# A column-sum kernel: loads folded to four rows and passed along a 24-row ring, shrinking loads at the end, 60 drains ahead of the vector work, and the last three rows read in two column blocks

## The chip, the cores and the metric

The kernel runs on one core of a Trainium2 chip. The metric is the device time of one execution in microseconds (us). Each run also lists its span, which is the time from the first to the last instruction that the profile counts, and the mean clock granted to the tensor engine. The time is about 2 us longer than the span (1.82 us in the profiled run of before). The difference between the two is called "outside the span" below.

In profile lines PE is the tensor engine's matmuls, PEld its weight loads, DVE VectorE, ACT ScalarE, and SP the sync engine, which issues all transfers here. SPq is the issuing itself.

## The reference

```python
def setup_inputs():
    batch, seq, dim = 32, 1024, 2048
    return {"grad_output": np.random.randn(batch, seq, dim).astype(np.float32)}

def reference(grad_output):
    return np.sum(grad_output, axis=(0, 1)).astype(np.float32)
```

A matrix of 32,768 x 2,048 floats, 268.4 MB, is read once and summed down to 2,048 numbers. On the chip 128 matrix rows, one for each partition, make one "row" of 1 MB in this document. The matrix has 256 such rows.

## The kernel before

```python
ROWS = 8
TAIL = (4, 2, 1)
# first column, columns, column group of 32 in PE's output
PIECES = ((0, 512, 1), (512, 512, 2), (1024, 512, 3), (1536, 256, 0), (1792, 256, 0))
...
io_pool = ctx.enter_context(tc.tile_pool(name="io", bufs=3))
nc.vector.memset(ones[:], 1.0)
...
def add_piece(b, src, stop=False):          # sum over the 128 partitions, into PSUM
    nc.tensor.matmul(sums[b], lhsT=ones[:], rhs=src, start=(b not in started), stop=stop)
...
for t in range(n_bulk):                     # 31 loads of 8 rows
    T = io_pool.tile([P, ROWS * D], fp32, tag="T", name=f"t{t}")
    nc.sync.dma_start(out=T[:], in_=src)
    n = ROWS * D // 2
    while n >= D:                           # 8 -> 4 -> 2 -> 1 rows on VectorE
        ...
        nc.vector.tensor_add(out=T[:, :n], in0=T[:, :n], in1=T[:, n : 2 * n])
        n //= 2
    if t:
        nc.vector.tensor_add(out=acc[:], in0=acc[:], in1=T[:, :D])

for i, m in enumerate(TAIL):                # 4, 2, 1 rows go to PE as they are
    nc.sync.dma_start(out=T[:, at * D : (at + m) * D], in_=src)
    for j in range(m):
        add_row(T[:, (at + j) * D : (at + j + 1) * D])
    at += m
add_row(acc[:])
for b, (lo, n, g) in enumerate(PIECES):     # the last row in five column pieces
    nc.sync.dma_start(out=dst, in_=flat[row : row + P, lo : lo + n])
    add_piece(b, dst, stop=True)
    if b in (0, 2, 4):
        nc.scalar.copy(out=res[:, lo : lo + n], in_=sums[b])
    else:
        nc.vector.tensor_copy(out=res[:, lo : lo + n], in_=sums[b])
nc.sync.dma_start(out=out[None, :], in_=res)
```

Lines are left out of this cut, also where no ... stands, and comments are added. The whole kernel follows.

Of the kernel before, what the change touches and what calls it, by code (L numbers as in the profile page):

```python
# [1 line left out]

# [4 lines left out]

P = 128
ROWS = 8  # L10
TAIL = (4, 2, 1)


PIECES = ((0, 512, 1), (512, 512, 2), (1024, 512, 3), (1536, 256, 0), (1792, 256, 0))


@with_exitstack
def kernel(
    ctx: ExitStack,
    tc: tile.TileContext,  # L20
    grad_output: bass.AP,
    out: bass.AP,
):
    nc = tc.nc
    fp32 = mybir.dt.float32
    D = out.shape[-1]
    flat = grad_output.rearrange("b s d -> (b s) d")
    R = flat.shape[0]
    n_bulk = (R // P - sum(TAIL) - 1) // ROWS
    assert (n_bulk * ROWS + sum(TAIL) + 1) * P == R  # L30

    io_pool = ctx.enter_context(tc.tile_pool(name="io", bufs=3))
    const_pool = ctx.enter_context(tc.tile_pool(name="const", bufs=1))
    psum_pool = ctx.enter_context(tc.tile_pool(name="psum", bufs=1, space=bass.MemoryType.PSUM))

    ones = const_pool.tile([P, 1], fp32)
    nc.vector.memset(ones[:], 1.0)  # L37
    warm = const_pool.tile([1, 1], fp32)
    nc.scalar.copy(out=warm[:], in_=ones[0:1, :])  # L39
    acc = const_pool.tile([P, D], fp32)  # L40
    sums = []
    for b, (lo, n, g) in enumerate(PIECES):
        bank = psum_pool.tile([P, 512], fp32, tag=f"ps{b}", name=f"ps{b}")
        sums.append(bank[32 * g : 32 * g + 1, :n])

    started = set()

    def add_piece(b, src, stop=False):
        nc.tensor.matmul(sums[b], lhsT=ones[:], rhs=src, start=(b not in started), stop=stop)  # L49
        started.add(b)  # L50

    def add_row(src):
        for b, (lo, n, g) in enumerate(PIECES):
            add_piece(b, src[:, lo : lo + n])

    row = 0
    for t in range(n_bulk):
        T = io_pool.tile([P, ROWS * D], fp32, tag="T", name=f"t{t}")
        src = flat[row : row + P * ROWS].rearrange("(p m) d -> p (m d)", p=P)
        nc.sync.dma_start(out=T[:], in_=src)  # L60
        row += P * ROWS
        n = ROWS * D // 2
        while n >= D:
            if t == 0 and n == D:
                nc.vector.tensor_add(out=acc[:], in0=T[:, :n], in1=T[:, n : 2 * n])  # L65
            else:
                nc.vector.tensor_add(out=T[:, :n], in0=T[:, :n], in1=T[:, n : 2 * n])  # L67
            n //= 2
        if t:
            nc.vector.tensor_add(out=acc[:], in0=acc[:], in1=T[:, :D])  # L70

    T = io_pool.tile([P, ROWS * D], fp32, tag="T", name="tail")
    at = 0
    for i, m in enumerate(TAIL):
        src = flat[row : row + P * m].rearrange("(p m) d -> p (m d)", p=P)
        nc.sync.dma_start(out=T[:, at * D : (at + m) * D], in_=src)
        row += P * m
        for j in range(m):
            add_row(T[:, (at + j) * D : (at + j + 1) * D])
        at += m  # L80
    add_row(acc[:])

    res = acc[0:1, :]
    for b, (lo, n, g) in enumerate(PIECES):
        dst = T[:, at * D + lo : at * D + lo + n]
        nc.sync.dma_start(out=dst, in_=flat[row : row + P, lo : lo + n])
        add_piece(b, dst, stop=True)
        if b in (0, 2, 4):
            nc.scalar.copy(out=res[:, lo : lo + n], in_=sums[b])  # L89
        else:  # L90
            nc.vector.tensor_copy(out=res[:, lo : lo + n], in_=sums[b])  # L91
    nc.sync.dma_start(out=out[None, :], in_=res)


# [1 line left out]
_INS = ['grad_output']  # L96
_OUTS = [((2048,), 'float32')]


# [23 lines left out]
```

## Time and profile before

| | before |
|---|---|
| time, median of the first 3 runs | 629.85 us (629.35 to 630.53) |
| span of the profiled run (timed 630.02) | 628.2 us |
| DMA packets, share of 16 engines' span | 99.0% |
| VectorE busy | 87% |
| last input landed, from the span's start | 624.16 us |

An input counts as landed when the last of the 16 DMA engines has reported its part of it. These times come from the semaphore records in the trace.

These are lines of the page of before: the busy times of part 1, the queues of part 3 (packets, megabytes, share of the 16 engines' time) and the chain of part 4.

```profile
span 628.2 us, 430 instructions
PE 10.6 (2%) x90; PEld 3.8 (1%) x90; DVE 547.6 (87%) x126; ACT 3.0 (0%) x5; POOL 0.2 (0%) x4
...
q1 hardware_dynamic: 5618, 268.45, 99.0%
q14 instruction: 1, 0.01, 0.0%
...
DMA 69%; DVE 28%; PE 2%; issue 0%; ACT 0%; SPq 0%; ACTq 0%
```

The DMA engines work nearly all the time (99.0%), and 268.4 MB pass through them whatever the kernel does. There is also one packet of another kind, on q14, which the page calls "instruction": 8,192 bytes at 240.15 us. It is called a fetch below and is taken to be VectorE's.

This is the view of groups by shape for VectorE in before. Its columns are the line, engine, operation, tiles, shapes and count, then the busy time and the mean ns of one, then the idle time before them.

```profile
L67 DVE TENSOR_TENSOR t<-t 128x8192 f32<-128x8192 f32 x31 | 269.5, 8692 | 71.8 <-DMA t<-in_grad_output_dram 71.8
L67 DVE TENSOR_TENSOR t<-t 128x4096 f32<-128x4096 f32 x31 | 137.2, 4425 | 1.1
L70 DVE TENSOR_TENSOR acc<-acc,t 128x2048 f32<-128x2048 f32 x30 | 68.8, 2292 | 1.0
L67 DVE TENSOR_TENSOR t<-t 128x2048 f32<-128x2048 f32 x30 | 68.8, 2292 | 1.0
```

One load costs VectorE 8.69 + 4.43 + 2.29 + 2.29 = 17.7 us, and a load lands every 19.35 us, so VectorE waits for the DMA with every load.

This is the end of the timeline of before (start, duration, engine, line, operation, tiles, count, and in brackets the idle time and what ended it).

```profile
617.62 2.29 DVE L67 TENSOR_TENSOR t<-t 128x2048 f32<-128x2048 f32 x1
617.63 4.98 PE L49 MATMUL ps<-tail,ones 128*1 128x512 f32 x50
619.95 2.29 DVE L70 TENSOR_TENSOR acc<-acc,t 128x2048 f32<-128x2048 f32 x1
622.42 1.05 PE L49 MATMUL ps<-acc,ones 128*1 128x512 f32 x10
623.28 1.63 PE L49 MATMUL ps<-tail,ones 128*1 128x512 f32 x10
624.34 1.57 ACT L89 COPY acc<-ps 1x512 f32<-1x512 f32 x3 [622.12 <-PE ps L49]
624.38 1.13 DVE L91 COPY acc<-ps 1x512 f32<-1x512 f32 x2 [2.14 <-PE ps L49]
625.93 0.33 SPq L92 DMA_DIRECT2D out_dram<-acc  x1
```

The accumulator is complete at 619.95 + 2.29 = 622.24 us. PE adds it, then the last row, whose last piece landed at 624.16, and ends at 624.91. Of the five result copies ScalarE makes three in a row. The output goes out at 625.93.

### The profile page before, as it was taken

The numbers are of one execution on the slowest core, as the hardware profiler recorded it, in microseconds if no ns is written. First come the engines' busy times: TensorE is split into PE (matmuls) and PEld (weight loads), VectorE is DVE, ScalarE is ACT, GpSimd is POOL, SyncE is SP. The second block draws the span as 40 slices with busy tenths as digits, with TensorE's granted clock in tenths as the row PEclk, the third lists the DMA queues.
The fourth block names the chain that finished last, engine by engine and source line by source line (L and its number), as shares of the span: only waits on it lengthen the run. The fifth ranks groups of instructions, "written<-read, shape, count | busy, mean of one in ns | idle before, by whom it ended". The sixth has DMA issues, their size and how long they took to land.

```text
span 628.2 us, 430 instructions
## 1 busy us (share of the span) xinstructions
PE 10.6 (2%) x90; PEld 3.8 (1%) x90; DVE 547.6 (87%) x126; ACT 3.0 (0%) x5; POOL 0.2 (0%) x4
## 2 busy tenths in 40 slices
PE   0000000000000000000000000000000000000006
PEld 0000000000000000000000000000000000000002
DVE  0578988889888899888898888988889988899886
ACT  0000000000000000000000000000000000000000
POOL 0000000000000000000000000000000000000000
PEclk9999999999999999999999999999999999999999
DMA  9999999999999999999999999999999999999996
GB/s 401 413 455 401 467 401 467 401 467 401 467 401 467 401 467 401 463 405 459 409 459 409 455 413 455 413 455 413 451 417 451 417 446 421 438 430 426 442 403 266
DMA packets 5619, 268.45 MB, mean 427 GB/s; under 512 B 625, under 2 KB 881, under 8 KB 1265
## 3 DMA queue, kind: packets, MB, share of 16 engines
q1 hardware_dynamic: 5618, 268.45, 99.0%
q14 instruction: 1, 0.01, 0.0%
HBM read 268.44 MB, written 0.01 MB: 427 GB/s over the span
## 4 chain that ended last, share of the span: by engine, by line
DMA 69%; DVE 28%; PE 2%; issue 0%; ACT 0%; SPq 0%; ACTq 0%
DMA t<-in_grad_output_dram 64%; DVE t L67 25%; DMA tail<-in_grad_output_dram 5%; DVE acc L70 4%; PE ps L49 2%; ACT acc L89 0%; SPq L60 0%; ACTq L118 0%
## 5 line engine op out<-in xcount | busy, mean ns | idle before, releaser
L67 DVE TENSOR_TENSOR t<-t 128x8192 f32<-128x8192 f32 (+2 forms) x92 | 475.4, 5167 | 73.9 <-DMA t<-in_grad_output_dram 71.8
L70 DVE TENSOR_TENSOR acc<-acc,t 128x2048 f32<-128x2048 f32 x30 | 68.8, 2292 | 1.0
L49 PE MATMUL ps<-tail,ones 128*1 128x512 f32 (+1 forms) x80 | 10.0, 627 | 614.3 <-DMA tail<-in_grad_output_dram 614.3
L49 PEld LDWEIGHTS ps<-tail,ones 128*1 128x1 f32 x80 | 3.5, 97 | 620.3 <-issue 617.4
L89 ACT COPY acc<-ps 1x512 f32<-1x512 f32 (+1 forms) x3 | 1.5, 506 | 622.2 <-PE ps L49 622.1
L91 DVE COPY acc<-ps 1x512 f32<-1x512 f32 (+1 forms) x2 | 1.1, 548 | 2.2 <-PE ps L49 2.1
L65 DVE TENSOR_TENSOR acc<-t 128x2048 f32<-128x2048 f32 x1 | 2.3, 2292 | 0.0
L39 ACT ACT_TABLE_LOAD x1 | 1.3, 1283 | 0.7 <-PEq L107 0.7
L49 PE MATMUL ps<-acc,ones 128*1 128x512 f32 (+1 forms) x10 | 1.1, 507 | 0.0
L37 DVE MEMSET ones<- 128x1 f32 x1 | 0.1, 59 | 0.8 <-PEq L107 0.8
L49 PEld LDWEIGHTS ps<-acc,ones 128*1 128x1 f32 x10 | 0.4, 82 | 0.4 <-DVE acc L70 0.2
L39 ACT COPY warm<-ones 1x1 f32<-1x1 f32 x1 | 0.2, 190 | 0.0
L107 POOL MEMSET const-bfloat16-1.0<- 128x1 bf16 x1 | 0.1, 101 | 0.0
L107 POOL MEMSET const-uint8-127<- 128x1 uint8 x1 | 0.1, 101 | 0.0
L107 POOL MEMSET const-float32-0.0<- 128x1 f32 x1 | 0.1, 98 | 0.2 <-issue 0.2
L107 POOL MEMSET const-float32-1.0<- 128x1 f32 x1 | 0.1, 98 | 0.0
## 6 DMA issues: line engine op xcount, KB each, us to landing
tail<-in_grad_output_dram SPq DMA_DIRECT2D x1, 4096.0 KB
tail<-in_grad_output_dram SPq DMA_DIRECT2D x1, 2048.0 KB, 35.1
tail<-in_grad_output_dram SPq DMA_DIRECT2D x1, 1024.0 KB, 37.1
tail<-in_grad_output_dram SPq DMA_DIRECT2D x3, 256.0 KB, 37.5
t<-in_grad_output_dram SPq DMA_DIRECT2D x31, 40.2
tail<-in_grad_output_dram SPq DMA_DIRECT2D x2, 128.0 KB, 28.6
out_dram<-acc SPq DMA_DIRECT2D x1, 8.0 KB
```

The lines of the kernel that those rows point to most:

```text
L37: nc.vector.memset(ones[:], 1.0)
L39: nc.scalar.copy(out=warm[:], in_=ones[0:1, :])
L49: nc.tensor.matmul(sums[b], lhsT=ones[:], rhs=src, start=(b not in started), stop=stop)
L65: nc.vector.tensor_add(out=acc[:], in0=T[:, :n], in1=T[:, n : 2 * n])
L67: nc.vector.tensor_add(out=T[:, :n], in0=T[:, :n], in1=T[:, n : 2 * n])
L70: nc.vector.tensor_add(out=acc[:], in0=acc[:], in1=T[:, :D])
L89: nc.scalar.copy(out=res[:, lo : lo + n], in_=sums[b])
L91: nc.vector.tensor_copy(out=res[:, lo : lo + n], in_=sums[b])
L107: nc = _bacc.Bacc("TRN2", target_bir_lowering=False, num_devices=1)
```

## The change

The intent has several parts. Each 8-row load is folded only to 4 rows, and the next load adds those 4 rows to itself, so that the running sum moves along a ring of 24 rows. After 23 loads the running sum is brought to 1 row. The loads then shrink (7, 6, 6, 5, 4, 2 and again 2 rows for VectorE, and twice 2 rows for PE, written as -2) to leave little work after the last landing. The last three rows are read as columns 0 to 1535 first, then columns 1536 to 2047, so that only two copies are left for the end. Sixty drains (in after's trace each takes 0.01 us and one follows another every 0.04 us) open VectorE's instruction stream. They are meant to bring the fetch, which before makes at 240.15 us, to a time before the stream of loads is at full speed. Three filler matmuls keep PE busy ahead of the end (3.31 us from 611.41 on in after).

```diff
-ROWS = 8
-TAIL = (4, 2, 1)
-PIECES = ((0, 512, 1), (512, 512, 2), (1024, 512, 3), (1536, 256, 0), (1792, 256, 0))
+RING = 24
+PLAN = (8,) * 27 + (7, 6, 6, 5, 4, 2, -2, 2, -2)
+LAST = (2, 1)
+N_WIDE = 23
+WIDE = 4
+DRAINS = 60
+FILLERS = 3
+LEFT = ((0, 512, 1), (512, 512, 2), (1024, 512, 3))
+RIGHT = ((1536, 256, 0), (1792, 256, 1))
 ...
-    nc.vector.memset(ones[:], 1.0)
+    for _ in range(DRAINS):
+        nc.vector.drain(fusable=False)
+    nc.gpsimd.memset(ones[:], 1.0)
 ...
+    load(row, 1, head[:])                   # one single row first
+    for m in PLAN:
+        at = take(abs(m))                   # the next place in the ring
+        load(row, abs(m), rows(at, abs(m)))
+        if m < 0:                           # rows for PE
+            for j in range(-m):
+                add((at + j) * D, LEFT + RIGHT)
+            continue
+        to = min(m, WIDE if n_fold < N_WIDE else 1)
+        ...
+            fold(run, height, to)           # the sum so far, to the height wanted
+            nc.vector.tensor_add(out=rows(at, to), in0=rows(at, to), in1=rows(run, to))
+        n_fold += 1
+        fold(at, m, to)
+        run, height = at, to
+        if n_fold == sum(m > 0 for m in PLAN):
+            for _ in range(FILLERS):
+                nc.tensor.matmul(junk[0:1, :], ...)
+    add(run * D, LEFT + RIGHT)
+    ...
+    for lo, hi, pieces in ((0, cut, LEFT), (cut, D, RIGHT)):
+        for i, m in enumerate(LAST):        # 2 rows, then 1 row, of these columns
+            load(first, m, ring[:, at : at + m * n], lo, hi)
+            ...
+    for k, (lo, n, g) in enumerate(LEFT + RIGHT):
+        ...                                 # copies: ACT, DVE, ACT, DVE, ACT
 (cuts marked with ...)
```

More of the change, by code (lines that the diff above doesn't have):

```diff
@@ L28 @@
     R = flat.shape[0]
-    n_bulk = (R // P - sum(TAIL) - 1) // ROWS
-    assert (n_bulk * ROWS + sum(TAIL) + 1) * P == R
-    io_pool = ctx.enter_context(tc.tile_pool(name="io", bufs=3))
+    assert (1 + sum(abs(m) for m in PLAN) + sum(LAST)) * P == R
     const_pool = ctx.enter_context(tc.tile_pool(name="const", bufs=1))
     psum_pool = ctx.enter_context(tc.tile_pool(name="psum", bufs=1, space=bass.MemoryType.PSUM))
+    ring = const_pool.tile([P, RING * D], fp32)
+    head = const_pool.tile([P, D], fp32)
@@ L36 @@
     ones = const_pool.tile([P, 1], fp32)
-    nc.vector.memset(ones[:], 1.0)
     warm = const_pool.tile([1, 1], fp32)
+    res = head[0:1, :]
+    for _ in range(DRAINS):
+        nc.vector.drain(fusable=False)
+    nc.gpsimd.memset(ones[:], 1.0)
     nc.scalar.copy(out=warm[:], in_=ones[0:1, :])
-    acc = const_pool.tile([P, D], fp32)
-    sums = []
-    for b, (lo, n, g) in enumerate(PIECES):
+    sums = {}
+    for b, (lo, n, g) in enumerate(LEFT + RIGHT):
         bank = psum_pool.tile([P, 512], fp32, tag=f"ps{b}", name=f"ps{b}")
-        sums.append(bank[32 * g : 32 * g + 1, :n])
+        sums[lo] = bank[32 * g : 32 * g + 1, :n]
@@ L46 @@
+    junk = psum_pool.tile([P, 512], fp32, tag="junk", name="junk")
     started = set()
-    def add_piece(b, src, stop=False):
-        nc.tensor.matmul(sums[b], lhsT=ones[:], rhs=src, start=(b not in started), stop=stop)
-        started.add(b)
-    def add_row(src):
-        for b, (lo, n, g) in enumerate(PIECES):
-            add_piece(b, src[:, lo : lo + n])
-    row = 0
-    for t in range(n_bulk):
-        T = io_pool.tile([P, ROWS * D], fp32, tag="T", name=f"t{t}")
-        src = flat[row : row + P * ROWS].rearrange("(p m) d -> p (m d)", p=P)
-        nc.sync.dma_start(out=T[:], in_=src)
-        row += P * ROWS
-        n = ROWS * D // 2
-        while n >= D:
-            if t == 0 and n == D:
-                nc.vector.tensor_add(out=acc[:], in0=T[:, :n], in1=T[:, n : 2 * n])
-            else:
-                nc.vector.tensor_add(out=T[:, :n], in0=T[:, :n], in1=T[:, n : 2 * n])
-            n //= 2
-        if t:
-            nc.vector.tensor_add(out=acc[:], in0=acc[:], in1=T[:, :D])
@@ L72, with add @@
-    T = io_pool.tile([P, ROWS * D], fp32, tag="T", name="tail")
-    at = 0
-    for i, m in enumerate(TAIL):
-        src = flat[row : row + P * m].rearrange("(p m) d -> p (m d)", p=P)
-        nc.sync.dma_start(out=T[:, at * D : (at + m) * D], in_=src)
-        row += P * m
-        for j in range(m):
-            add_row(T[:, (at + j) * D : (at + j + 1) * D])
-        at += m
-    add_row(acc[:])
-    res = acc[0:1, :]
-    for b, (lo, n, g) in enumerate(PIECES):
-        dst = T[:, at * D + lo : at * D + lo + n]
-        nc.sync.dma_start(out=dst, in_=flat[row : row + P, lo : lo + n])
-        add_piece(b, dst, stop=True)
-        if b in (0, 2, 4):
-            nc.scalar.copy(out=res[:, lo : lo + n], in_=sums[b])
-        else:
-            nc.vector.tensor_copy(out=res[:, lo : lo + n], in_=sums[b])
+    def add(at, pieces, base=0, stop=False):
+        for lo, n, g in pieces:
+            x = at + lo - base
+            nc.tensor.matmul(
+                sums[lo], lhsT=ones[:], rhs=ring[:, x : x + n], start=(lo not in started), stop=stop
+            )
+            started.add(lo)
@@ new lines, with take, load, rows @@
+    row = pos = 0
+    def take(m):
+        nonlocal pos
+        if pos + m > RING:
+            pos = 0
+        at = pos
+        pos += m
+        return at
+    def load(first, m, dst, lo=0, hi=D):
+        src = flat[first : first + P * m].rearrange("(p m) d -> p m d", p=P)[:, :, lo:hi]
+        nc.sync.dma_start(out=dst.rearrange("p (m d) -> p m d", m=m), in_=src)
+    def rows(at, m):
+        return ring[:, at * D : (at + m) * D]
+    def fold(at, height, to):
+        while height > to:
+            k = min(height - to, height // 2)
+            nc.vector.tensor_add(out=rows(at, k), in0=rows(at, k), in1=rows(at + height - k, k))
+            height -= k
@@ new lines @@
+    load(row, 1, head[:])
+    row += P
+    run = height = None
+    n_fold = 0
+    for m in PLAN:
+        at = take(abs(m))
+        load(row, abs(m), rows(at, abs(m)))
+        row += P * abs(m)
+        if m < 0:
[3 more added lines that the diff above has]
+        to = min(m, WIDE if n_fold < N_WIDE else 1)
+        if n_fold == 0:
+            nc.vector.tensor_add(out=rows(at, 1), in0=rows(at, 1), in1=head[:])
+        else:
+            to = min(to, height)
+            fold(run, height, to)
[5 more added lines that the diff above has]
+            for _ in range(FILLERS):
+                nc.tensor.matmul(junk[0:1, :], lhsT=ones[:], rhs=rows(at + m - 1, 1)[:, :512], start=True, stop=True)
@@ new lines @@
+    add(run * D, LEFT + RIGHT)
+    at = take(sum(LAST)) * D
+    cut = RIGHT[0][0]
+    for lo, hi, pieces in ((0, cut, LEFT), (cut, D, RIGHT)):
+        first = row
+        for i, m in enumerate(LAST):
+            n = hi - lo
+            load(first, m, ring[:, at : at + m * n], lo, hi)
+            first += P * m
+            for j in range(m):
+                add(at, pieces, base=lo, stop=(i == len(LAST) - 1 and j == m - 1))
+                at += n
+    for k, (lo, n, g) in enumerate(LEFT + RIGHT):
+        if k in (0, 2, 4):
+            nc.scalar.copy(out=res[:, lo : lo + n], in_=sums[lo])
+        else:
+            nc.vector.tensor_copy(out=res[:, lo : lo + n], in_=sums[lo])
```

## The prediction

> **What bounds the kernel now.** The DMA stream. The queue table gives its packets 99.0% of 16 engines' span of 628.2 us. In the packet records a 64 KB packet takes 2.420 us, 27.1 GB/s per engine or 433 for 16, from 1.77 to 623.72 us, and an 8-row load lands every 19.35 us. [...] VectorE is busy 87%, but in the groups view a load costs it 8.69+4.43+2.29+2.29 = 17.7 us against 19.35: it waits 1.6 us for each load and isn't the limit, although the chain of waits passes through it (28%).
>
> Only three things can change: the start (1.77 us), unevenness among the 16 engines, and the 4.0 us after the last landing (624.16 us).
>
> **What the change does, costed.**
> 1. Folding to 4 rows and passing on: 8.69+8.69 = 17.4 us per load. Off the critical path: 0. A slot comes free about 8.7 us after the next load lands; the following load streams for 10 us more, so the queue never empties.
> 2. Going to 1 row costs 4.43+2.29 us once; VectorE falls about 5 us behind and regains 1.6 us per load before the shrinking loads (2.42 us of streaming per row), each of which costs it slightly less than it streams. The last vector fold then ends some 7 us before the last landing; in before the accumulator is ready at 622.24 us and holds PE until 624.9.
> 3. Tail: in before the last ACT copy starts at 625.54 us, 0.64 us after its sum was ready, behind another copy. Afterwards ACT and VectorE copy the last two sums in parallel. Estimate: -0.6 us, less 0.1 to 0.3 if PE is at its slow pace there.
> 4. The 60 drains: in before an 8 KB instruction packet at 240.15 us runs on one DMA engine, and the packet beside it takes 3.08 us. From then on the sixteenth engine lands 0.75 us behind the fifteenth; earlier it was 0.06 us. [...] here it costs about 0.7 us, because the queue never empties. The drains should pull this fetch into the first microseconds. Estimate: -0.4 us (0 to -0.75). They run in the first 22 us, when VectorE idles.
> 5. More and smaller packets: from 2.420 us for 64 KB and 0.314 for 8 KB I work out 10 ns per packet; some 32 more per engine and two more loads cost +0.35 us.
>
> Sum: about -0.6 us, a span of 627.6. Timed: **629.1 us**, 8 times in 10 between 628.2 and 630.0. Chances: faster by over 2% 0.01, within 2% 0.98, slower by over 2% 0.01.
>
> **What would show it right.** DMA share about 99%; 8-row landings 19.35 us apart; no instruction packet after the first few microseconds, and the last two engines within 0.2 us; from the last landing to the end 3.3 to 3.6 us; VectorE waiting about 2 us per load; the last copies in parallel.
>
> **What would make it wrong.** A second instruction fetch late in the run (VectorE has 191 instructions, before 135); a slot wait that empties the queue; part-row pieces streaming slower than estimated; chip to chip scatter, as large as the effect (629.35 to 630.53).

The sum: -0.6 for the copies, -0.4 for the fetch and +0.35 for packets come to -0.65, the "about -0.6 us" that takes the span from 628.2 to 627.6. An estimate: at the 433 GB/s that the text works out from its packets, 268.4 MB take about 620 us. That only three things can change is thus the author's estimate too. PE's slow pace, which step 3 allows for, is in the trace of before: a matmul of 512 columns takes 1.06 us there up to the row at 617.63 us, and 0.59 us from 618.98 on.

## The result

| | before | after |
|---|---|---|
| time, median (range) of 4 runs each, same chip | 629.64 us (629.35 to 630.53) | 630.72 us (630.59 to 631.14) |
| ratio of after to before, 95% interval | | 1.0016 (0.9999 to 1.0033) |
| profiled run: time, span | 630.02, 628.2 us | 630.59, 628.4 us |

A ratio here is the mean time of one kernel's fast runs over the mean of the other's fast runs of the same rounds, so it is not quite the ratio of the medians beside it. Within 2%, the two kernels are the same. Yet the prediction gave 629.1 us and a range from 628.2 to 630.0, and every run of after lies above it. Instead of gaining about 0.7 us (629.85 to 629.1) the change lost about 0.6 us between the profiled runs, and about 1 us between the medians.

The lines of the page of after that answer to those of before:

```profile
span 628.4 us, 484 instructions
PE 16.1 (3%) x86; PEld 3.4 (1%) x86; DVE 544.0 (87%) x89; ACT 3.0 (0%) x5; POOL 0.3 (0%) x5
...
q1 hardware_dynamic: 6162, 268.45, 99.0%
q14 instruction: 2, 0.02, 0.0%
...
DMA 54%; DVE 43%; PE 1%; issue 0%; another core or an unknown queue 0%; SPq 0%; ACT 0%; DVEq 0%
```

The stream is as full as before, 99.0%. The q14 line now has two instruction fetches instead of one: at 29.20 us, and at 628.20 us at the end of the span. A further one, at 630.06, lies past the end. Before has one near its end too, at 628.55 us, which falls just past its span and so isn't counted; the one that is new is that at 630.06.

The groups of VectorE in after, by shape:

```profile
L93 DVE TENSOR_TENSOR ring<-ring 128x8192 f32<-128x8192 f32 x27 | 234.7, 8692 | 0.9
L114 DVE TENSOR_TENSOR ring<-ring 128x8192 f32<-128x8192 f32 x22 | 191.2, 8692 | 49.3 <-DMA ring<-in_grad_output_dram 49.3
L93 DVE TENSOR_TENSOR ring<-ring 128x4096 f32<-128x4096 f32 x8 | 35.4, 4426 | 0.3
```

A wide load costs 8.69 + 8.69 = 17.4 us, as the prediction says, and VectorE waits about 2 us for each (49.3 us over 22 loads, one of them the 8.7 us of the first). The 8-row loads land 19.35 us apart, as they do in most of before. So the large middle of the run is as foreseen, and what differs lies at the end.

The end of the timeline of after:

```profile
606.70 5.28 PE L68 MATMUL ps<-ring,ones 128*1 128x512 f32 x20 [606.70 <-DMA ring<-in_grad_output_dram]
610.51 2.29 DVE L114 TENSOR_TENSOR ring<-ring 128x2048 f32<-128x2048 f32 x1
611.41 3.31 PE L120 MATMUL junk<-ring,ones 128*1 128x512 f32 x6
...
615.16 2.29 DVE L114 TENSOR_TENSOR ring<-ring 128x2048 f32<-128x2048 f32 x1
616.30 2.74 PE L68 MATMUL ps<-ring,ones 128*1 128x512 f32 x20 [1.58 <-DMA ring<-in_grad_output_dram]
617.49 2.29 DVE L93 TENSOR_TENSOR ring<-ring 128x2048 f32<-128x2048 f32 x1
619.84 5.32 PE L68 MATMUL ps<-ring,ones 128*1 128x512 f32 x40 [0.79 <-DVE ring L93]
623.90 1.66 ACT L136 COPY head<-ps 1x512 f32<-1x512 f32 x3 [621.68 <-PE ps L68]
623.94 0.69 DVE L138 COPY head<-ps 1x512 f32<-1x512 f32 x1 [4.16 <-PE ps L68]
624.80 0.41 DVE L138 COPY head<-ps 1x256 f32<-1x256 f32 x1 [0.18 <-PE ps L68]
625.58 0.33 SPq L139 DMA_DIRECT2D out_dram<-head  x1
```

VectorE's last fold ends at 617.49 + 2.29 = 619.78 us. PE then works without a pause from 619.84 to 625.16 and is never seen to wait for the last landings, the last of which came at 623.87. The table below puts both profiled runs together.

| piece, us | before | after | difference |
|---|---|---|---|
| start of the span to the last input landed | 624.16 | 623.87 | -0.29 |
| then to the end of the last matmul | 0.75 | 1.29 | +0.54 |
| then to the issue of the output | 1.02 | 0.42 | -0.60 |
| then to the output landed | 1.39 | 1.40 | 0.01 |
| then to the end of the span | 0.93 | 1.46 | +0.53 |
| outside the span | 1.82 | 2.19 | +0.37 |
| sum | 630.07 | 630.63 | +0.56 |

The sums stand within 0.05 us of the two times (630.02 and 630.59), because the spans are rounded to 0.1 in the list of runs. The gain that was sought is there: -0.60 us from the copies. It was more than given back in three other places, of which the prediction's sum contains none.

The -0.29 us of the first line is not a gain of the change. In the profiled run of before all engines were a little slower from 31 to 100 us (64 KB packets of up to 2.63 us, where 2.42 is the median): four loads landed 19.55, 19.55, 19.46 and 19.40 us apart, which is about 0.6 us in all over the usual 19.35. Two variants of before below do not show this. Why it happened in that run stays open.

### The profile page after: what moved, and what is told of

It is laid out like the page before. It is cut to its first block, busy times and chain, and to the rows that moved or that the text cites. A ratio compares the mean times of both kernels' runs of the same rounds, so it can differ in the third digit from the quotient of the medians.

```text
span 628.4 us, 484 instructions
## 1 busy us (share of the span) xinstructions
PE 16.1 (3%) x86; PEld 3.4 (1%) x86; DVE 544.0 (87%) x89; ACT 3.0 (0%) x5; POOL 0.3 (0%) x5
## 4 chain that ended last, share of the span: by engine, by line
DMA 54%; DVE 43%; PE 1%; issue 0%; another core or an unknown queue 0%; SPq 0%; ACT 0%; DVEq 0%
DMA ring<-in_grad_output_dram 54%; DVE ring L93 23%; DVE ring L114 21%; PE ps L68 1%; SPq L85 0%; ACT head L136 0%; DVEq L114 0%
## 5 line engine op out<-in xcount | busy, mean ns | idle before, releaser
L93 DVE TENSOR_TENSOR ring<-ring 128x8192 f32<-128x8192 f32 (+3 forms) x53 | 324.1, 6116 | 1.8
L114 DVE TENSOR_TENSOR ring<-ring 128x8192 f32<-128x8192 f32 (+1 forms) x33 | 216.5, 6559 | 49.7 <-DMA ring<-in_grad_output_dram 49.3
L68 PE MATMUL ps<-ring,ones 128*1 128x512 f32 (+1 forms) x80 | 13.3, 599 | 609.1 <-DMA ring<-in_grad_output_dram 608.3
L110 DVE TENSOR_TENSOR ring<-ring,head 128x2048 f32<-128x2048 f32 x1 | 2.3, 2292 | 25.4 <-DMA ring<-in_grad_output_dram 25.4
L68 PEld LDWEIGHTS ps<-ring,ones 128*1 128x1 f32 x80 | 3.0, 87 | 618.9 <-issue 613.5
L136 ACT COPY head<-ps 1x512 f32<-1x512 f32 (+1 forms) x3 | 1.5, 507 | 621.8 <-PE ps L68 621.7
L120 PE MATMUL junk<-ring,ones 128*1 128x512 f32 x6 | 3.3, 696 | 0.0
```

What stands on the lines that cost most here:

```text
L68: nc.tensor.matmul(sums[lo], lhsT=ones[:], rhs=ring[:, x : x + n], start=(lo not in started), stop=stop)
L93: nc.vector.tensor_add(out=rows(at, k), in0=rows(at, k), in1=rows(at + height - k, k))
L110: nc.vector.tensor_add(out=rows(at, 1), in0=rows(at, 1), in1=head[:])
L114: nc.vector.tensor_add(out=rows(at, to), in0=rows(at, to), in1=rows(run, to))
L120: nc.tensor.matmul(junk[0:1, :], lhsT=ones[:], rhs=rows(at + m - 1, 1)[:, :512], start=True, stop=True)
L136: nc.scalar.copy(out=res[:, lo : lo + n], in_=sums[lo])
```

## The experiments

Six theories were tested. They carry letters below.

- **A.** VectorE has 191 instructions with the drains. Its instruction stream makes a pause and a fetch at fixed places (in after one pause of 0.455 us ends at 25.405 us and a fetch is at 29.20), and the drains move one of these places to just after the end of the span, where it prolongs the time outside the span (2.19 us instead of 1.82).
- **B.** The sync engine pauses before its 82nd instruction (627.139 to 627.584 us in after). In after that instruction is one of the closing waits and stands after the output has landed.
- **C.** VectorE is late with the shrinking loads, its last row comes at 619.78 us, and PE has not caught up when the last piece lands.
- **D.** The drains don't remove the instruction fetch from the stream, they only move it, and a fetch anywhere costs the same lag at the end.
- **E.** PE gets half its clock for a while after it has idled (0.5 for 3.413 us after 2.16 us of idle time in a_d0), and for after, which idles for 1.58 us, it is close whether that happens.
- **F.** The fifth accumulator moved to column group 1, which the first one uses too, and this changes what a row costs PE (1.29 us in after, 0.86 in a_g0).

The rival of them all is that after's difference is scatter between chips and runs. Each call of runs shared its chip and its runs of before, so every variant is set against those.

### Theories A and D: the drains taken away, and put into before

```diff
-DRAINS = 60
+DRAINS = 0          # a_d0: after without drains
```
```diff
+    for _ in range(60):                     # b_d60: before with drains
+        nc.vector.drain(fusable=False)
     nc.vector.memset(ones[:], 1.0)
```

> The changed kernel without its 60 vector drains. Theory A (the drains only add VectorE instructions, and the extra block of instructions they need is fetched in the epilogue): the time outside the profiled span falls from 2.15-2.2 us to about 1.8 us, the instruction packet near 630 us after the span is gone, timed about 630.4 us. The in-stream instruction packet moves from 29 us to the middle of the run and still puts one DMA engine 0.7-0.8 us behind, so the span stays 628.2-628.6. Rival (the drains pay for themselves, as the author of the change meant): the last landing becomes 0.3-0.7 us later without them, and the time rises to 631 or more.

> The kernel before plus the 60 drains alone. Theory A: the time outside the span rises from 1.8 to about 2.15 us and a second instruction packet stands after the span; the in-stream packet moves towards the start of the run (about 22-30 us) and the lag of 0.7-0.8 us on one engine begins there; span unchanged at 628.2, ratio to before about 1.0005. Rival (drains pull the fetch out of the stream): the lag is gone, the span falls by about 0.7 us.

| | median, us | ratio to before (95%) | outside the span | fetch in the stream at | sixteenth engine behind the fifteenth at the end |
|---|---|---|---|---|---|
| before, same chip (9 runs) | 629.61 | 1 | 1.73 to 1.81 | | |
| after (its own chip) | 630.72 | 1.0016 | 2.14 to 2.20 | 29.20 us | 0.73 us |
| a_d0 | 630.27 | 1.0011 (0.9998 to 1.0025) | 1.75 to 1.79 | 416.25 us | 0.83 us |
| b_d60 | 629.74 | 1.0001 (0.9988 to 1.0013) | 1.74 to 1.82 | 7.51 us | 0.57 us |

In the profiled run of before the fetch is at 240.15 us. Up to then the sixteenth engine lands its part of each load 0.15 and soon 0.06 us behind the fifteenth, and from then on about 0.75 us behind, to the end. In after the fetch is at 29.20 us and the lag is about 0.8 us from the third landing on. With and without drains, in both kernels, the fetch comes at another time and the lag appears and stays. So the drains moved the fetch, and the 0.4 us that the prediction gave them is not there. The first half of theory D is shown.

Taking the drains out of after brought the time outside the span from about 2.17 back to about 1.77 us in all five runs, and the instruction fetch that after shows at 630.06 us, past the end of its span, is gone. That the drains cost after this time is shown. The traces also show the delay itself: after the span the semaphores are updated in blocks, and the block of numbers 156 to 206 begins 0.78 us past the span's end in before, a_d0 and b_d60, but 1.15 or 1.16 us past it in after and in the four variants with its VectorE program (a_sp4, a_f0, a_f6, a_g0). The fetch at 630.06 us starts only 1.62 us past the end, so the packet is not what delays the block; a pause of VectorE would fit, but can't be seen there.

Theory A needs a refinement, because b_d60 has 195 instructions on VectorE, and 2.15 us outside the span were expected for it, but 1.78 were measured, although two instruction packets do start past its span (at 628.08 and 628.22 us). In b_d60 the pause sits inside the closing barrier instead, where the engines wait for one another: VectorE's instructions there leave a gap from 627.094 to 627.546 us, and the span's end follows the landing of the output 1.14 us later instead of 0.93. This gap stands before the 192nd instruction that the trace records. (It records two fewer than each program has.) After pauses in the same way before its 64th, 128 earlier, and ends with its 189th, so that its next such place would lie just behind the end. That fits both kernels, but was not tested further. Nor is the time outside the span fully explained: a_skip and a_nofetch below take 1.97 to 2.06 and 1.99 to 2.25 us there, although their block begins at 0.78 us, and for a_nofetch 1.8 had been expected. Why stays open.

### Theory B: the sync engine's pause moved

```diff
         n_fold += 1
+        if n_fold == 1:                     # a_sp4: after with 4 drains on the sync engine
+            for _ in range(4):
+                nc.sync.drain(fusable=False)
```
```diff
         nc.sync.dma_start(out=T[:], in_=src)
+        if t == 1:                          # b_sp5: before with 5 of them
+            for _ in range(5):
+                nc.sync.drain(fusable=False)
```

> The changed kernel with 4 drains on the sync engine's own program early on. Theory B (the 0.45 us pause of the sync engine after the output has landed is a pause at a fixed place in its instruction stream, the 82nd instruction): the pause moves to before the wait for the output, where it is hidden; from the landing of the output to the end of the span 0.9-1.0 us instead of 1.42, span about 627.9. Rival (the pause belongs to what that instruction waits for, a DMA or ScalarE): it stays before the same instruction, 0.45 us, and the span stays 628.4.

> The kernel before plus 5 sync-engine drains early on. Theory B (a pause of 0.45 us before the 82nd instruction of the sync engine's program): the pause, which in before stood inside the closing barrier and cost some 0.3 us there, moves behind the wait for the output; from the landing of the output to the end 0.55-0.65 us instead of 0.88, ratio to before 0.9995. Rival: unchanged 0.88 us.

The instructions of the sync engine show the pause directly. In after a closing wait ends at 627.139 us and the next one begins at 627.584, without anything to wait for. In a_sp4 the same pause of about 0.45 us stands four instructions earlier in the program, at 626.606 to 627.069, while the output is still under way. From the output's landing to the end of the span a_sp4 then takes 1.00 us, where after takes 1.46. This was expected and is shown: +0.46 us of after's +0.53 are this pause. In all 16 profiled runs whose sync engine has that many instructions it idles for 0.42 to 0.46 us before the same one, the 80th that the trace records and the 82nd of the program.

In a_sp4 the spans are 627.8, 628.1 and 628.1 us in the three runs at full clock, against 628.4, 628.5 and 628.6 in after. The other two runs have 628.4 and 628.7 at a mean clock of 0.997, which is theory E's business. Its median is 630.27 us, 1.0011 times before.

In b_sp5 the pause moved as well, to 625.968 to 626.391 us, but from the output's landing to the end it still takes 0.84 us, where 0.55 to 0.65 had been expected. In before the pause lies in the closing barrier from 627.474 to 627.918 us and seems to be mostly hidden there: removing it gained 0.09 us, and the other engines' part of the barrier would take the rest of that time anyway, which was not shown. The size was missed. b_sp5 ran at 629.52 us, against 630.10 for before on that chip, with a ratio of 0.9994 (0.9982 to 1.0007).

### Theory C: less vector work at the end

After folds its 4-row load (the 32nd) to one row, and the two-row loads too. This variant leaves out some of it. Its result is wrong, and only its times are used.

```diff
-        fold(at, m, to)
+        if m > 5 or n_fold < 28:            # a_skip: wrong sum on purpose
+            fold(at, m, to)
```

> The changed kernel without the folds inside its last four folded loads (5, 4, 2 and 2 rows): a wrong sum on purpose; PE's work, the loads and the packets are the same. Theory C (VectorE, late in the shrinking loads by up to 9 us, hands over its last row at 619.8 us and so makes PE late): the last row is ready near 614 us, the last matmul ends 0.7-0.9 us after the last landing instead of 1.29, span 0.4-0.6 us shorter, about 627.9. Rival (PE's own queue at the end, 6 rows in 5 us, sets it): the last matmul still ends about 1.3 us after the last landing and the span stays 628.4.

These are the last instructions of a_skip in the timeline.

```profile
616.28 6.69 PE L68 MATMUL ps<-ring,ones 128*1 128x512 f32 x48 [1.74 <-DMA ring<-in_grad_output_dram]
...
623.25 1.46 PE L68 MATMUL ps<-ring,ones 128*1 128x256 f32 x12 [0.28 <-DMA ring<-in_grad_output_dram]
624.75 0.41 DVE L139 COPY head<-ps 1x256 f32<-1x256 f32 x1 [1.02 <-PE ps L68]
...
625.22 0.33 SPq L140 DMA_DIRECT2D out_dram<-head  x1
```

Here PE waits 0.28 us for the last landing, which after's PE does not, and ends at 624.71 us, 0.87 us after the landing (623.84), where after needs 1.29. Its five spans are 628.1 or 628.2 us, against 628.4 to 629.0 in after. The rival, that PE's work on the last pieces themselves takes 1.29 us, falls. Theory C is shown, and costs after 0.3 to 0.5 us. The landing times show how it comes about:

| load (rows) | landed, us | first add, us | lag, us |
|---|---|---|---|
| 27th (8) | 528.82 | 529.26 | 0.44 |
| 28th (7) | 545.77 | 547.10 | 1.34 |
| 29th (6) | 560.30 | 562.81 | 2.51 |
| 30th (6) | 574.83 | 576.38 | 1.55 |
| 31st (5) | 586.95 | 589.96 | 3.01 |
| 32nd (4) | 596.67 | 601.40 | 4.73 |
| 33rd (2) | 601.56 | 610.51 | 8.95 |
| next of VectorE (2) | 611.36 | 615.16 | 3.80 |

The 4-row load keeps VectorE busy from 601.40 to 610.51 us, which is 9.11 us. It took 9.72 us to stream, so by the prediction's yardstick it fits. But in those 9.11 us only the next load arrives, and that one has 2 rows and takes 4.89 us. The lag grows to 4.73 + 9.11 - 4.89 = 8.95 us, just as measured.

### The instruction fetch measured by itself (theory D)

```diff
-DRAINS = 60
+DRAINS = 0
-            nc.vector.tensor_add(out=rows(at, to), in0=rows(at, to), in1=rows(run, to))
+            if n_fold % 2 == 0 or n_fold > 26:
+                nc.vector.tensor_add(out=rows(at, to), in0=rows(at, to), in1=rows(run, to))
         n_fold += 1
-        fold(at, m, to)
+        if n_fold > 28:                     # a_nofetch: wrong sum on purpose
+            fold(at, m, 1) if m == 2 else None
```

With this VectorE has 56 instructions, and the trace shows no fetch during the stream.

> The changed kernel without drains and with most vector adds left out, so that VectorE's whole program has 56 instructions: a wrong sum on purpose, the same loads and PE work. Theory D (the instruction fetch costs 0.7-0.8 us at the end because one DMA engine stays behind): no instruction packet inside the stream, the last engine within 0.1 us of the fifteenth, the last landing at 623.1-623.3 instead of 623.87, span 0.6-0.8 us below that of the run without the tail folds (628.1), so 627.3-627.5, and 1.8 us outside the span. Rival (the lag is there anyhow, or the end is set by PE and not by the slowest engine): the last landing stays near 623.8 or the span stays above 628.

The queues in the page of a_nofetch:

```profile
span 626.9 us, 339 instructions
...
q1 hardware_dynamic: 6162, 268.45, 99.2%
HBM read 268.44 MB, written 0.01 MB: 428 GB/s over the span
```

There is no q14 line, and the share of q1 rose to 99.2%. The sixteenth engine ends 0.02 us behind the fifteenth, and the last landing is at 623.12 us, against 623.84 in a_skip, which loads the same in the same order and does fetch. One fetch during the stream therefore costs 0.72 us at the end, and the second half of theory D is shown. The two runs are from different chips, but their fifteenth engines end within 0.04 us of each other (623.09 and 623.13), so the chip is not what makes the difference. The three runs at full clock have spans of 626.9 us, the other two 628.0 at 0.997. The median is 629.07 us, 0.9989 times before (0.9977 to 1.0002). The sync engine has only 77 instructions here, so theory B's pause is gone too, and part of the shorter span is that: 1.0 us from the landing of the output to the end.

### Theory E: the fillers

```diff
-FILLERS = 3
+FILLERS = 0         # a_f0; and 6 in a_f6
```

> The changed kernel without its 3 filler matmuls. Theory E ([...] in the changed kernel this makes the difference between spans of 628.4 and 629.0-629.3): without fillers PE idles longer before the last rows, the clock is at half in the last 8 us in most runs, the last matmul ends about 2.0-2.3 us after the last landing instead of 1.3, spans 629.0-629.6 and mean clock below 1.0 in most runs. Rival (PE's pace is not what sets the end): spans stay 628.4-628.6.

> The changed kernel with 6 fillers instead of 3, so that PE has work from the first pair of rows until the next pair lands. Theory E (PE's clock window): no run with a mean clock below 1.0, all spans 628.2-628.6, where the changed kernel itself had one of 629.0 and two of its variants had half of their runs at 628.7-629.3. Rival (the slow spans come from elsewhere): spans spread as before, 628.2-629.3.

In the view of windows the column PEclk is the granted clock. It stands behind the busy times of the five engines, and before the DMA share and the GB/s. First after from 614 to 622 us:

```profile
614.00:618.00 4.00, 2.42 (x19) 0.46 (x18) 3.93 (x3) 0.00 (x0) 0.00 (x0) 1.00 0.98 406
618.00:622.00 4.00, 3.21 (x27) 0.74 (x26) 1.78 (x1) 0.00 (x0) 0.00 (x0) 1.00 1.01 399
```

Then a_f0:

```profile
614.00:618.00 4.00, 1.68 (x11) 0.25 (x13) 3.93 (x3) 0.00 (x0) 0.00 (x0) 0.62 0.96 400
618.00:622.00 4.00, 4.00 (x22) 0.90 (x19) 1.83 (x1) 0.00 (x0) 0.00 (x0) 0.53 1.01 402
```

And the profiled run of a_d0, which is after without drains and has the three fillers:

```profile
614.00:618.00 4.00, 1.84 (x15) 0.42 (x17) 3.93 (x3) 0.00 (x0) 0.00 (x0) 0.92 1.00 413
618.00:622.00 4.00, 4.00 (x25) 1.02 (x21) 1.92 (x1) 0.00 (x0) 0.00 (x0) 0.65 1.01 400
```

Without fillers PE ran at half clock for about 6.8 of these 8 us (worked out from the PEclk of 0.62 and 0.53), and its last matmul ended at 626.91 us, 3.0 us after the landing, instead of 1.29 (2.0 to 2.3 had been expected). The five runs have spans from 628.9 to 630.2 us and a mean clock of 0.995 to 0.997, and the median is 631.96 us, 1.0026 times before (1.0013 to 1.004). With six fillers all five runs had a mean clock of 1.0 and spans of 628.3 to 628.5 us, a median of 630.59 and a ratio of 1.0008 (before on that chip: 630.02). This kernel is otherwise after, and lies behind before on another chip by the same 0.6 us. All its runs lie above all nine of before there (629.49 to 630.39), as after's four do on their chip. That speaks against the rival of scatter, although the intervals of both ratios contain 1. Theory E is shown, in both directions.

The clock records give the length of one such stretch: in a_d0 the clock is 0.5 from 617.370 to 620.783 us, which is 3.413 us, and in a_sp4 from 617.417 to 620.831, again 3.41. PE had idled from 614.27 to 616.43 us in a_d0, 2.16 us, and from 614.12 to 616.27 in a_sp4. In the profiled run of after it idled for 1.58 us (614.72 to 616.30) and kept its clock. Every stretch in the clock records that ends within a span is a whole multiple of 3.413 us, such as the 10.24 us in a_best1 below, which are three of them. The stretches at full clock that run past the end of the span are too: 10.240 us from 618.620 on in before, and 17.067 us, five of them, from 612.604 on in after.

The length of a gap alone does not decide. In its profiled run a_nofetch idled for 2.18 us (613.33 to 615.51), longer than a_d0, and kept its full clock. The traces show a difference if windows of 3.413 us are counted off from the clock records, which is an estimate from these records alone: in a_d0 all 2.16 us of idle time fall into one window, as do 2.15 us in a_sp4, 2.11 in a_best2 and 2.16 in b_best, and each time the next window was at half clock. In a_nofetch a window ends at 613.69, in the middle of the gap, so that at most 1.82 us fall into one. The place of the windows against the program differs between traces (one begins at 612.604 us in after, one at 617.370 in a_d0, 1.4 windows later). If it also differs from run to run of one kernel, which one trace of each can't show, this would explain why a_d0 has spans of 628.2 and twice 628.5 us at clock 1.0, and 629.2 and 629.3 at 0.997. No run tested it by itself.

A mean clock of 1.0 does not cover PE's start. The first clock record of after is at 612.60 us, while PE begins at 606.70 and takes 5.28 us there for the 20 recorded matmuls of two rows that take 2.74 us from 616.30 on.

### Theory F: the column group

```diff
-RIGHT = ((1536, 256, 0), (1792, 256, 1))
+RIGHT = ((1536, 256, 0), (1792, 256, 0))    # a_g0
```

> The changed kernel with its fifth accumulator back on the PE column group that the kernel before used (with the fourth, instead of with the second). Theory F (with 512+256 columns on one group a whole row costs PE 1.29 us at full clock, with 256+256 on one group 0.86): whole rows follow at 0.86 us again, so the left pieces of the last three rows start about 0.4 us earlier; but a right half row then costs 0.86 instead of 0.43 us, the last matmul ends 1.8-2.2 us after the last landing instead of 1.29, span 628.9-629.3. Rival (the group doesn't matter, matmuls of one row overlap anyhow): no change, 628.4.

With both right pieces in group 0, as before has them, a whole row costs PE 0.86 us, where after's order costs 1.29, but the right half of a row costs 0.86 where after's costs 0.43. The last matmul ended at 626.04 us, 2.16 us after the landing. The four spans are 629.2, 629.2, 629.3 and 630.2 us, and the median of 631.43 is 1.0025 times before. This was expected. The change's grouping is right for the end of the run, where only right halves are left to do. It makes the rows before them slower, which sharpens theory C.

### Attempts to mend both kernels

The first attempt has no drains, four drains on the sync engine, and more rows for PE.

```diff
-PLAN = (8,) * 27 + (7, 6, 6, 5, 4, 2, -2, 2, -2)
+PLAN = (8,) * 27 + (7, 6, 5, -2, 4, -2, 3, -2, 2, -3)   # a_best1
-N_WIDE = 23, DRAINS = 60, FILLERS = 3
+N_WIDE = 20, DRAINS = 0, FILLERS = 5
+        if n_fold == 1: (4 sync drains, as in a_sp4)
```

> The changed kernel mended in the places that the runs point to: no drains, 4 sync-engine drains early on, a tail of 7, 6, 5, -2, 4, -2, 3, -2, 2, -3 rows (minus: rows that PE adds) in which VectorE keeps up, 20 wide folds, 5 fillers. If theories A, B, C and E hold: VectorE's last row is ready 9-10 us before the last landing, the last matmul ends 0.8-0.9 us after it, output landing to end 0.9-1.0 us, 1.8 us outside the span, span 627.5-627.9, timed 629.3-629.7: at most 0.2 us better than before. If only packets count: 630.

It failed: 632.06 us, 1.0027 times before. VectorE was on time, as wanted, but PE idled from 613.9 to 616.5 us and ran at half clock from 616.345 to 619.759. (Two longer stretches at half clock, 10.24 us each, lie before 610 us and make up most of its low mean clock of 0.981.) There was also an instruction fetch on another queue, a q8 line of 0.02 MB, at 620.17 us. It appears only in the variants with the most PE instructions (the pages of a_best3b with 102 matmuls and of b_best with 100 have it, those of before with 90 and of after with 86 do not) and is taken for PE's own. After it two DMA engines instead of one were behind, and the last of them by 1.4 us instead of 0.9. The last landing was at 624.57 us and the last matmul ended at 627.30.

The second and third differ from it in the plan and the fillers.

```diff
-PLAN = (8,) * 27 + (7, 6, 6, 5, 4, 2, -2, 2, -2)
+PLAN = (8,) * 27 + (7, 6, 6, 6, 4, -3, 2, -2)           # a_best2, FILLERS = 3
-N_WIDE = 23, DRAINS = 60                                # a_best3, FILLERS = 6
+N_WIDE = 20, DRAINS = 0
+        if n_fold == 1: (4 sync drains, as in a_sp4)
```

> The changed kernel without drains, with 4 sync-engine drains, 20 wide folds and a tail of 7, 6, 6, 6, 4, -3, 2, -2 rows, 3 fillers: VectorE on time (last row ready about 7 us before the last landing), PE busy earlier and at full clock. If A, B, C and E hold: last matmul 0.85-0.95 us after the last landing, span 627.4-627.8, timed 629.2-629.6. If PE's clock falls again in the last window: spans of 628.5 or more in some runs.

> The second mended version of the changed kernel with 6 fillers instead of 3, so that PE has no gap between 611 and 618 us. If the account is complete: clock 1.0 in all runs, all spans 627.4-627.8 (the mended version before it showed 627.5 and 627.7 in its two runs with full clock), the last matmul 0.85-1.0 us after the last landing, 1.8-1.9 us outside the span, timed 629.3-629.6, ratio to before 0.9990-0.9995. If something else is left: spans above 628 at full clock.

a_best2 has two runs at full clock, with spans of 627.5 and 627.7 us, and three at 0.997 with 628.5 and 628.6. Its median is 630.44 us, 1.0003 times before, and is the time of the very run whose span was 627.5: that run spent 2.94 us outside the span, where the other four spent 1.79 to 2.03. Why stays open. With three more fillers, a_best3 has spans of 627.5 to 627.7 us in four runs, which is the span of 627.6 that the prediction gave for after. Its fifth run took 695.16 us, which counts as slow and is left out of the ratio of 0.9997. It happened to be the profiled one. Every matmul in it took 1.3 to 3.1 us. The 1.0 that the list of runs gives as its clock says nothing, because its trace holds no clock record at all. To see whether the kernel does this, it ran once more, unchanged:

> The same kernel as a_best3 once more, for a trace in the normal state. If the account is complete: clock 1.0, span 627.4-627.8, last landing near 623.9, last matmul 0.85-1.0 us after it, from the output's landing to the end 0.9-1.0 us, ratio to before 0.9992-0.9998. If the state of 695 us belongs to this kernel and not to chance: it shows again in one or more of the five runs.

None of these five runs did: 629.39 to 629.58 us with a median of 629.48, against 629.89 (629.33 to 630.36) for before on the same chip, a ratio of 0.9994 (0.998 to 1.0007). The end of its timeline:

```profile
623.38 1.46 PE L68 MATMUL ps<-ring,ones 128*1 128x256 f32 x12 [0.26 <-DMA ring<-in_grad_output_dram]
624.87 0.41 DVE L141 COPY head<-ps 1x256 f32<-1x256 f32 x1 [1.00 <-PE ps L68]
624.92 0.36 ACT L139 COPY head<-ps 1x256 f32<-1x256 f32 x1 [0.59 <-PE ps L68]
625.37 0.33 SPq L142 DMA_DIRECT2D out_dram<-head  x1
```

PE waits 0.26 us for its last data in this run, and the last matmul ends at 624.84 us, 0.87 us after the landing at 623.97. The output landed at 626.75 us, and the span ended 0.95 us later. What is left is the lag of the sixteenth engine, 0.68 us. The nine normal runs of this kernel lie between 629.38 and 629.59 us, and the 45 runs of before that were timed beside the variants lie between 629.23 and 630.62. Its scatter is smaller, but the interval of the ratio contains 1, so it is not proven that it beats before.

Before was given the same ideas: a last bulk load of 7 rows, the last row in a tile of its own so that its loads need not wait, copies after all adds, and five sync drains.

```diff
-TAIL = (4, 2, 1)
+TAIL = (4, 2, 2)                            # b_best; (4, 2, 1, 1) in b_best2
+BULK = (8,) * 30 + (7,)
+LAST = 1
 ...
+    L = io_pool.tile([P, ROWS * D], fp32, tag="T", name="last")
-        dst = T[:, at * D + lo : at * D + lo + n]
+        dst = L[:, lo : lo + n]
         add_piece(b, dst, stop=True)
+    for b, (lo, n, g) in enumerate(PIECES):
         (copies as they were)
```

> The kernel before with its tail mended: last folded load of 7 rows, tail of 4, 2, 2 rows on PE and one row in five pieces, 5 sync-engine drains early on. Expected from its trace: the accumulator is ready about 5 us before the last landing instead of 2, PE is not behind when the pieces of the last row land, the first copies start about 0.4 us before the last landing, the output is issued 1.4 us after it instead of 1.77, and 0.3 us less in the closing barrier: span 0.6-0.7 us shorter, ratio to before 0.9989. Rival (the tail of before is set by the last piece alone): only the 0.3 us of the barrier, 0.9995.

> The mended tail of the kernel before with PE rows landing as 4, 2, 1, 1 and one row in five pieces, so that PE does not idle over 1.6 us: clock 0.999-1.0 in all runs, accumulator ready about 5 us before the last landing, output issued about 1.4 us after it instead of 1.77, 0.3 us less in the closing barrier, span 627.4-627.8 where before has a mean of 628.1, ratio to before 0.9988-0.9993. If PE's clock falls again: spans of 630.

The last part of the timeline of b_best:

```profile
621.30 2.42 PE L50 MATMUL ps<-tail,ones 128*1 128x512 f32 x20 [2.33 <-DMA tail<-in_grad_output_dram]
623.45 1.97 PE L50 MATMUL ps<-acc,ones 128*1 128x512 f32 x10
625.16 1.46 PE L50 MATMUL ps<-last,ones 128*1 128x512 f32 x10
```

Its PE had nothing to do for 2.33 us (618.97 to 621.30), ran at half clock from 622.55 to 625.97, and ended at 626.62: 632.30 us, 1.0028 times before. That one run of it that kept its full clock took 630.59. In b_best2 two rows are loaded one by one, so the idle time is 1.45 us (619.90 to 621.35), the clock stays at 0.999 to 1.0, and the spans are 627.5 to 628.0 us. It ran at 629.73 us, 0.9997 times before. The output was issued 1.75 us after the last landing, where 1.4 had been expected, so the hoped-for gain was missed: PE is still behind with the two single rows and the accumulator until about 623 us when the pieces of the last row come.

## Why the prediction was wrong

**What was right.** The DMA stream bounds both kernels (99.0% in both, 19.35 us per load). Outside it before has about 8 us, 1.3% of its time (1.77 us ahead of the first packet, and all that follows 623.72), so without a faster stream nothing over 2% was to be had. No run shows a faster one: the earliest last landing reported here is 623.12 us (a_nofetch). Folding to four rows is off the critical path: VectorE waits about 2 us per load. After the change to one row VectorE's lag was 4.98 us at the 24th landing, and by the 27th it was back to 0.44, as foreseen. The drains themselves are hidden: they ran in the first 3.1 us, while VectorE had nothing to do. Step 3 was right in size: from the last matmul to the issue of the output it takes 0.42 us instead of 1.02, thus -0.60.

**The step that failed first: "The drains should pull this fetch into the first microseconds. Estimate: -0.4 us".** The reading of the lag as the cost of a fetch was right, and a_nofetch measures it as 0.72 us. That it is pulled to where it does no harm was wrong. It came at 29.20 us, not during the drains, with the stream at full speed, and the sixteenth engine never catches up on a queue that never empties. Even early is not early enough: in b_d60 the fetch did come in the first microseconds, at 7.51 us, when VectorE had nothing to do, and the lag was there from the first landing to the last (0.59 and 0.57 us). Measured gain: 0, the lag at the end being 0.68 us before and 0.73 after.

**What the drains cost was not in the sum.** The prediction names "a second instruction fetch late in the run" as a risk and expects it in the stream. What the runs show is a delay after the span, +0.37 us, removed by a_d0; the fetch that comes with it starts only after the delay.

**Step 2, "each of which costs it slightly less than it streams. The last vector fold then ends some 7 us before the last landing".** It ended 4.1 us before (619.78 against 623.87). Each load's work was compared with that load's own streaming, where it has to fit into the streaming of the next, smaller one. The cost at PE is +0.54 us in the profiled runs. a_skip gets 0.42 of it back, 0.87 us instead of 1.29.

**A term that was missing: the sync engine's pause.** +0.53 us between the landing of the output and the end of the span, of which a_sp4 takes 0.46 back. Nothing in the prediction looks at where an engine's instruction count puts such a pause.

**PE's clock at the end.** The prediction allows "0.1 to 0.3 if PE is at its slow pace there". In the profiled run of after the recorded clock was full from 612.60 us on. In variants it costs up to about 1.7 us after the last landing (a_f0, 3.0 instead of 1.29) and splits the runs of one kernel into two groups. It explains none of the difference in the profiled runs, but the fourth run of after, with 631.14 us, 0.997 and a span of 629.0, lies apart like those.

**Step 5, "some 32 more per engine and two more loads cost +0.35 us".** This was too large. The fifteenth of the 16 engines' reports, which the fetch does not delay, comes at 623.09 to 623.25 us in after and six variants with its loads, and at 623.05 and 623.02 in b_d60 and b_sp5. This is about 0.1 us, hardly to be told from scatter.

**The prediction's own check.** It asked for the last two engines within 0.2 us and for 3.3 to 3.6 us from the last landing to the end of the span. The profiled run of after has 0.73 and 4.57.

**The sum again.** Predicted were -0.6 for the copies, -0.4 for the fetch and +0.35 for packets, about -0.6 us together. Measured are -0.60 for the copies, 0 for the fetch, about +0.1 for packets, +0.54 at PE, +0.53 in the closing waits and +0.37 outside the span: +0.9 us. Before's slower stretch of about 0.6 us lies on top of this in its profiled run, which leaves +0.3, and +0.56 was measured. The missing 0.2 to 0.3 us are within the scatter of the last landing, which is between 623.55 and 623.97 us in the profiled runs of before's variants. The predicted time took only 1.5 us for the part outside the span (629.1 - 627.6), where the profiled run of before has 1.82, so 0.3 us of the miss is this slip. The predicted span of 627.6 us was reached by a_best3, with four things mended at once: no drains, the sync pause moved, VectorE in time, and PE kept busy.

## What to carry to other kernels

When a saturated stream bounds a kernel, cost the last microseconds as their own sum: last landing, last matmul, output, closing waits, and the part outside the span, and count the instructions of each engine, because the sync engine's pause of 0.42 to 0.46 us came before its 82nd instruction in all 16 profiled runs that have one. A shrinking tail works only if each load's work fits into the streaming of the next, smaller load: here 9.11 us of work met 4.89 us of streaming, and the lag grew to 8.95 us. An engine that idles before the end should be kept busy if its clock depends on it: here PE's clock fell to 0.5 for 3.413 us after 2.16 us of idle time (a_d0; 2.18 us in a_nofetch did not do it), three spare matmuls were not always enough (one of four runs of after at 0.997), and six were (a_f6, 1.0 in all five runs).

## What the runs leave open

- Where a fetch starts. It came during the 47th recorded instruction of VectorE in before (240.15 us) and during the 65th in after (29.20 us). The packets on q14 during the stream are of 8,192 bytes, the one on q8 of 16,384. From the 64th to the 192nd instruction, before which VectorE paused in after and in b_d60, it is 128, but that one fetch brings 128 instructions was not shown. One fetch during the stream put one DMA engine 0.57 to 0.83 us behind at the end (b_d60 and a_d0), and cost 0.72 us there (a_nofetch against a_skip).
- What the pauses of about 0.45 us in an engine's own instruction stream are: the sync engine's from 627.139 to 627.584 us in after, VectorE's from 24.950 to 25.405 us in after and from 627.094 to 627.546 in b_d60.
- How VectorE's instruction count changes the time outside the span: 2.14 to 2.20 us in after, 1.75 to 1.79 in a_d0.
- What the run of 695.16 us was, in which matmuls took 1.3 to 3.1 us and no clock was recorded. It came once in ten runs of that kernel.
